# Output projection of an encoder layer: second norm scaled on ScalarE by halves, early weight operands spread evenly, an own bank for the mixed transposition's second half

## Chip, core and metric

The kernel runs on one core of a Trainium2 chip. The metric is the device time of one execution in microseconds, lower is better. Engines are named as in the profile: PE is TensorE's matrix multiplier and PEld its weight load, DVE is VectorE, ACT is ScalarE, POOL is GpSimd, SP is SyncE, which here issues nearly all loads (a q behind a name, as in SPq, means the engine's sequencer and its queue of DMA issues).

## The reference

One encoder layer over 1280 tokens (256 of a prompt, 1024 of a sample), width 1024, feed-forward width 2816, all in fp32:

```
proj = rmsnorm(x, attn_norm_g) @ w_in
a = mla_group(...)                 # latent attention, 8 heads, 512 columns
b = na_group(...)                  # neighbourhood attention, 8 heads, 512 columns
mix = concat(rmsnorm(a, mla_out_g), rmsnorm(b, na_out_g))
x = x + mix @ w_o                  # output projection
h2 = rmsnorm(x, ffn_norm_g)        # second norm
x = x + (silu(h2 @ w_gate) * (h2 @ w_up)) @ w_down
y = rmsnorm(x, final_norm_g)
```

## The kernel before

Every fp32 product is made of three matmuls on operands split into a high part (rounded to fp32r) and a low part (the rest): high x high, high x low, low x high. This is `mm3`, lines 111 to 113. The feed-forward products use a fast matrix multiplication scheme with 20 block products for each block of weights; their operands are sums and differences of 2 x 4 blocks of weights (W side) and of the activations (S and X tiles).

The change lies in the stage between attention and the feed-forward, and in the first block of feed-forward products. Tokens come in NT = 10 tiles of 128. The loop `for t in range(NT)` interleaves work of several tiles:

- `mix_in(t + 2)` loads a tile of attention results (`m`, from `a_d` and `b_d`) through SP, squares its two halves on ACT (L881, with the sums of squares), gets the reciprocal root `rm` on POOL (`rstd_of`, L90 and L92) and scales both halves on POOL (L886). `mixed[0]` is the last of these instructions.
- `mix_T(t + 1)` transposes the scaled tile on PE in two halves of four 128 x 128 blocks (L898) into the PSUM tile `trm`, of which there is one buffer. Each half is read by ACT for the high part (L900) and by DVE for the low part (L901) of `mT`.
- `out_proj(t)` does 16 groups of three matmuls (two halves of 512 columns, eight blocks of the inner dimension) into the PSUM tiles `po`; as each half ends, DVE adds the residual (L930, `added[0]`). Between its groups stand, by `between`, the transpositions of the next tile's `mT` (after groups 1 and 5) and those of the previous tile's second norm (after groups 10 and 13).
- `ffn_in(t)` squares the sum `x` on ACT (L941), stores `x` to `xm_d`, gets `rh` on POOL (`normed[0]`), and scales `x` into `h2` on DVE in one instruction of 1024 columns (L944, `scaled[0]`; `h2` has the tile name `m`). Its inner `half(q)`, called a tile later from `out_proj`, transposes four blocks each (L960): half 0 into `trh`, evicted by DVE (L964) with the gain, half 1 into a junk bank of the pool `pm0` ("M" in the profile, `junk[2]`) or for the last two tiles into `trm`, evicted by ACT (L970).
- `early_operands` is a generator that makes 18 weight operands of the first feed-forward block ahead of time on POOL: sums (L1067), the high part (L1072), the low part (L1074) into one of two buffers `wr`; SP stores each to `wop_d` (`load_r(*job)`, L77), at the start of the next iteration, or at once when three are pending. `next(early, None)` makes one. The raw weights (`wraw`) come in three parts in the first three iterations.
- `JOBS`, `FIRST` and `SECOND` are sums and splits of the S and X tiles on ACT and DVE (L985, L987, L995), placed behind named instructions.

Engine order: SP's queue and, from t = 1 to the end of the first feed-forward block, PE's order are the program's (`manual_schedule`). The other engines get their order from a planner that takes instructions by program order and its own estimate of when they are ready; `tc.issue_after(ins)` holds the instructions of a block behind `ins` on the same engine. Each engine executes its list in order.

After the loop, the first feed-forward block runs 20 steps (`SEQ0`), each with one product for G (gate) and one for U (up). At step `at` SP loads the operands for step `at + 3` into the ring `wr`; raw weights of the second block are loaded by `load_raw(1, ...)`. `xm_in(i)`, called within step 3, does the two halves of the last tile's transpositions; after the second it releases the pool `po` and opens `pm1`, from which the fifth step takes its banks. The pool `pm0` has four banks named M0, used as junk or transposition targets in the loop and by the products later.

Of the kernel before, what the change touches and what calls it, by code (L numbers as in the profile page):

```python
# [12 lines left out]
F32 = mybir.dt.float32  # L13
F32R = mybir.dt.float32r
AF = mybir.ActivationFunctionType
ALU = mybir.AluOpType
# [3 lines left out]
P = 128  # L20
# [20 lines left out]
def encoder_trunk(ctx: ExitStack, tc: tile.TileContext, x_tm, x_T, g_attn, w_c, w_v, w_qk,  # L41
# [3 lines left out]
    nc = tc.nc  # L45
# [10 lines left out]
    def pool(name, bufs=1, side=None, space=None):  # L56
        kw = {"reuse_waits": "tile"}
        if side:
            kw["side"] = side
        if space:  # L60
            kw["space"] = space
        return tc.alloc_tile_pool(name=name, bufs=bufs, **kw)

    def load(out, in_):
        nc.sync.dma_start(out=out, in_=in_)

    def store(out, in_):
        nc.scalar.dma_start(out=out, in_=in_)
# [7 lines left out]
    def load_r(out, in_):  # L76
        nc.sync.dma_start(out=out.bitcast(F32), in_=in_.bitcast(F32))  # L77
# [10 lines left out]
    def rstd_of(out, ss, n):  # L88
        w = out.shape[1]
        nc.gpsimd.tensor_scalar(out=out, in0=ss, scalar1=1.0 / n, scalar2=EPS,  # L90
                                op0=ALU.mult, op1=ALU.add)
        return nc.gpsimd.tensor_tensor(out=out, in0=out, in1=mhalf[:, 0:w], op=ALU.pow).ins  # L92
# [70 lines left out]
    def load_x(t):  # L163
        x = rx.tile([P, D], F32, name="x", bufs=2)
        load(x, x_tm[t * P:(t + 1) * P, :])
        return x
# [684 lines left out]
    po = pool("po", space=PSUM, side="right")  # L851
# [6 lines left out]
    def load_wo(n, pl, nm):  # L858
        raws = pl.tile([P, 2, D], F32, name=nm)
        for j in range(2):  # L860
            kc, raw = 2 * n + j, raws[:, j]
            load(raw, w_o[kc])
            nc.gpsimd.tensor_scalar(out=raw, in0=raw, scalar1=gm[:, kc:kc + 1], scalar2=1.0,
                                    op0=ALU.mult, op1=ALU.mult)
            wt = rw.tile([P, 2, D], F32R, name=f"wo{kc}")
            split_w(wt[:, 0], wt[:, 1], raw)
            wo.append(wt)
# [23 lines left out]
    def mix_T(t, mn):  # L891
        mT = (rt1 if t % 2 else rt0).tile([P, 2, KC, P], F32R, name=f"mT{t % 2}")

        def half(q):
            tr = po.tile([P, 4, P], F32, name="trm", bufs=1)
            for i in range(4):
                kc = 4 * q + i
                nc.tensor.transpose(tr[:, i], mn[:, kc * P:(kc + 1) * P], ident)  # L898
            hi, lo = mT[:, 0, 4 * q:4 * q + 4], mT[:, 1, 4 * q:4 * q + 4]
            last_split[0] = nc.scalar.copy(out=hi, in_=tr).ins  # L900
            last_low[0] = nc.vector.tensor_sub(out=lo, in0=tr, in1=hi).ins  # L901

        return mT, half
# [31 lines left out]
    normed, added = [None], [None]  # L935

    def ffn_in(t, x):
        h2 = rm.tile([P, D], F32, name="m", bufs=3)
        ss = rm.tile([P, 1], F32, name="ssh", bufs=2)
        r = rm.tile([P, 1], F32, name="rh", bufs=2)  # L940
        nc.scalar.activation(h2, x, AF.Square, accum_out=ss)  # L941
        store(xm_d[t], x)
        normed[0] = rstd_of(r, ss, D)
        scaled[0] = nc.vector.tensor_scalar(out=h2, in0=x, scalar1=r, scalar2=1.0, op0=ALU.mult,  # L944
                                            op1=ALU.mult).ins
        cuts, a = [], t * P
        while a < (t + 1) * P:
            j = a // XC
            e = min((j + 1) * XC, (t + 1) * P)
            cuts.append((j, slice(a - j * XC, e - j * XC), slice(a - t * P, e - t * P)))  # L950
            a = e

        def half(q):
            if q and t < NT - 2:
                tr = junk[2].rearrange("p (a b) -> p a b", a=4)
            else:
                tr = po.tile([P, 4, P], F32, name="trm" if q else "trh", bufs=1)
            for i in range(4):
                kc = 4 * q + i
                tp = nc.tensor.transpose(tr[:, i], h2[:, kc * P:(kc + 1) * P], ident)  # L960
            for j, to, of in cuts:
                if q == 0:
                    for k in range(2):
                        ev[0] = nc.vector.tensor_mul(  # L964
                            out=X[k, j][:, :, to], in0=tr[:, 2 * k:2 * k + 2, of],
                            in1=gf[:, 2 * k:2 * k + 2].unsqueeze(2).to_broadcast(
                                [P, 2, of.stop - of.start])).ins
                else:
                    for i in range(4):
                        nc.scalar.activation(X[2 + i // 2, j][:, i % 2, to], tr[:, i, of],  # L970
                                             AF.Copy, scale=gf[:, 4 + i:5 + i])
            return tp.ins

        return half

    ev, scaled = [None], [None]
# [56 lines left out]
    def load_raw(fp, i):  # L1033
        load(raw[:, i], src[i][fp])

    pm = [pool("pm0", space=PSUM)]
    for n, (pl, nm) in enumerate(((rw, "wo4"), (rw, "wo5"), (rw, "wo6"), (rt0, "mT0"))):
        load_wo(n, pl, nm)
    junk = [None] + [pm[0].tile([P, 512], F32, name="M0", bufs=4) for _ in range(2)]
    cur, half = mix_T(0, mix_in(0))  # L1040
    half(0)
    half(1)
# [36 lines left out]
    early = early_operands()  # L1079
# [3 lines left out]
    def behind_now(ins, job):  # L1083
        if job:
            with tc.issue_after(ins):
                job()
# [3 lines left out]
    for t in range(NT):  # L1090
        if t == 1:
            pe_order.enter_context(tc.manual_schedule(engines={mybir.EngineType.SP,
                                                               mybir.EngineType.PE}))
        if t + 2 < NT:
            with tc.issue_after(last_split[0]):
                coming = mix_in(t + 2)
        x = load_x(0) if t == 0 else x_next
        x_next = load_x(t + 1) if t + 1 < NT else None
        for job in kept:
            load_r(*job)  # L1100
        kept.clear()
        if t < 3:
            k = (slice(4, 6), slice(0, 4), slice(6, 8))[t]
            for i in range(2):
                load(raw[:, i, k], src[i][0][:, k])
        with tc.issue_after(mixed[0]):
            for _ in range(2 if 1 < t < 6 else 1):
                next(early, None)
        jobs = JOBS.get(t, (None,) * 3)
        halves_[0] = t < NT - 1  # L1110
        if t == NT - 1:
            with tc.issue_after(scaled[0]):
                for job in SECOND[4:5] + SECOND[6:]:
                    job()
        between = {}
        if t + 1 < NT:
            nxt, half_m = mix_T(t + 1, ahead)

            def second_m(half_m=half_m, jobs=jobs):
                half_m(1)  # L1120
                behind_now(last_low[0], jobs[0])

            between[1] = lambda: half_m(0)
            between[5] = second_m
        if t:
            def first_h(half=last_half, jobs=jobs):
                half(0)
                behind_now(ev[0], jobs[2])
                if t == 8:
                    behind_now(ev[0], jobs[3])  # L1130

            between[10 if t < 9 else 8] = first_h
            between[13 if t < 9 else 11] = lambda half=last_half: half(1)
        if t < NT - 1:
            between[7] = lambda jobs=jobs: behind_now(added[0], jobs[1])
        out_proj(t, cur, x, between)
        if t == NT - 1:
            break
        last_half = ffn_in(t, x)
        with tc.issue_after(normed[0]):  # L1140
            next(early, None)
            if t == 8:
                third_2(gps, slice(0, 168))
        cur, ahead = nxt, coming
# [14 lines left out]
    def xm_in(q):  # L1159
        last_half(q)  # L1160
        if q == 0:
            return
        for p_ in reversed(r3):
            p_.release()
        po.release()
        pm.append(pool("pm1", space=PSUM, side="right"))
        l4.append(pool("l4t"))
# [163 lines left out]
    for at in range(20):  # L1331
        if at and at + 3 < 20:
            load_r(ring[(at + 3) % 4], wop_d[SEQ0[at + 3][0]])
        if at in (5, 7):
            load_raw(1, at == 7)
        if at in BUILD:
            with tc.issue_after(evicted[0]):
                build_S(BUILD[at])
        w = ring[at % 4]
        for i, C in enumerate((G, U)):  # L1340
            product(C, chains[i], written[i], SEQ0, at, (w[:, 0, i], w[:, 1, i]), BANK.get(at))
            if at == 3:
                xm_in(i)
    pe_order.close()
    gate(G, 1)
# [438 lines left out]
```

## Time and profile before

| | us |
|---|---|
| three runs | 1592.95, 1595.09, 1591.53 (median 1592.95) |
| the profiled execution | 1593.86 |
| its span in the profile | 1591.8 |
| PE busy | 1559.4 (98% of the span) |
| DVE, ACT, POOL busy | 1016.4, 760.2, 766.4 |

The page gives one profiled execution. The times in its rows are counted from the start of the span. A row of the timeline gives start, length, engine, line, operation, tile written and tiles read, shape, number of instructions merged, and in brackets the idle time before it and what ended it. A row of the waits gives the waiting engine, tile and line, what it waited for, the total, how often, and the longest.

### The profile page before, as it was taken

To read this page: it belongs to the slowest core of one execution; us is meant where nothing else is said; L and a number is where in the kernel's file an instruction comes from. 1 tells how busy PE (TensorE), PEld (TensorE's weight loads), DVE (VectorE), ACT (ScalarE), POOL (GpSimd) and SP (SyncE) were. 2 spreads that over 40 slices of the span, in tenths; PEclk is the share of its full clock that TensorE was granted. 3 is DMA by queue.
4 is the path that set the end of the run, shared out by engine and by line. 5 is a ranking of instruction groups with operands and counts; after the bars stand their busy time and mean duration, and the time that the engine had idled before them with its cause. 6 is when DMAs were issued, how large, how long until landed. Compare 5 with 4: busy or idle time off the path is not lost.

```text
span 1591.8 us, 23991 instructions
## 1 busy us (share of the span) xinstructions
PE 1559.4 (98%) x8560; PEld 1394.9 (88%) x8560; DVE 1016.4 (64%) x1656; ACT 760.2 (48%) x1552; POOL 766.4 (48%) x961
## 2 busy tenths in 40 slices
PE   8999999999999999999999999999999999999998
PEld 8888789998888888877799999999999988888886
DVE  5754035556777777535698766566766666886676
ACT  6534144455777777633344344444334353443334
POOL 4632235544211119359626888788888871010002
PEclk9999999999999999999999999999999999999999
DMA  8626022243101021285573232223322237843434
GB/s 288 206 73 167 17 54 64 38 169 107 32 15 30 20 97 38 69 274 202 193 247 110 85 103 78 100 88 111 111 77 98 83 131 286 292 120 99 151 104 157
DMA packets 118022, 190.38 MB, mean 120 GB/s; under 512 B 34960, under 2 KB 65424, under 8 KB 115344
## 3 DMA queue, kind: packets, MB, share of 16 engines
q1 hardware_dynamic: 85216, 162.64, 31.4%
q10 hardware_dynamic: 31872, 23.14, 4.6%
q0 software_dynamic: 816, 3.08, 0.5%
q8 instruction: 67, 1.10, 0.3%
q14 instruction: 51, 0.42, 0.1%
HBM read 128.92 MB, written 59.90 MB: 119 GB/s over the span
## 4 chain that ended last, share of the span: by engine, by line
PE 83%; POOL 6%; DMA 3%; DVE 3%; ACT 3%; issue 2%; SPq 0%; POOLq 0%; ACTq 0%; DVEq 0%
PE M L113 10%; PE M L111 10%; PE M L112 10%; PE d L111 6%; PE d L113 6%; PE d L112 6%; PE o L789 4%; PE tp L779 3%; PE na_o L513 3%; PE pj L111 2%; PE pj L112 2%; PE pj L113 2%; PE S L111 2%; PE S L113 2%; PE S L112 2%
## 5 line engine op out<-in xcount | busy, mean ns | idle before, releaser
L1242 DVE TENSOR_TENSOR C<-M,C 128x428 f32<-128x428 f32 (+1 forms) x263 | 151.0, 594 | 144.0 <-issue 68.1
L1023 POOL TENSOR_TENSOR wr<-wt,wr 128x512 fp32r<-128x512 f32 (+1 forms) x106 | 148.9, 1405 | 67.4 <-ACT wr L1021 67.3
L1021 ACT CAST wr<-wt 128x512 fp32r<-128x512 f32 (+1 forms) x106 | 63.2, 599 | 134.2 <-PE M L112 123.7
L111 PE MATMUL M<-s,wr 128*128 128x428 f32 x352 | 125.9, 358 | 1.2 <-ACT x L970 1.2
L112 PE MATMUL M<-s,wr 128*128 128x428 f32 x352 | 125.4, 356 | 0.0
L113 PE MATMUL M<-s,wr 128*128 128x428 f32 x352 | 125.3, 357 | 0.0
L101 DVE TENSOR_TENSOR PT<-tp,PT 128x512 fp32r<-128x512 f32 (+1 forms) x144 | 93.4, 658 | 35.4 <-ACT PT L100 34.2
L1244 ACT COPY C<-M 128x428 f32<-128x428 f32 (+1 forms) x128 | 63.3, 514 | 84.6 <-PE M L113 84.6
L111 PE MATMUL M<-x,wr 128*128 128x428 f32 x264 | 94.2, 357 | 1.5 <-DVE C L1242 1.4
L100 ACT CAST PT<-tp 128x512 fp32r<-128x512 f32 (+1 forms) x144 | 79.4, 568 | 33.4 <-PE tp L779 30.2
L802 POOL TENSOR_TENSOR ob<-ob 128x128 f32<-128x128 f32 x40 | 18.4, 461 | 158.5 <-ACT ob L799 155.1
L771 DVE TENSOR_REDUCE mm<-S 128x1 f32<-128x1024 f32 (+1 forms) x80 | 85.0, 1062 | 13.8 <-PE S L113 12.3
L113 PE MATMUL M<-x,wr 128*128 128x428 f32 x264 | 91.5, 357 | 0.5 <-POOL wr L1023 0.3
L112 PE MATMUL d<-SE 128*128 128x512 f32 (+1 forms) x238 | 91.7, 387 | 0.0
L111 PE MATMUL d<-SE 128*128 128x512 f32 (+1 forms) x238 | 89.6, 388 | 0.0
L113 PE MATMUL d<-SE 128*128 128x512 f32 (+1 forms) x238 | 89.6, 387 | 0.0
L1284 ACT CAST SE<-as 128x640 fp32r<-128x640 f32 x58 | 42.2, 727 | 94.8 <-issue 57.2
L773 ACT ACTIVATE ex<-S,mm 128x1024 f32<-128x1024 f32 (+1 forms) x80 | 79.8, 998 | 14.9 <-DVE mm L771 13.6
L779 PE MATMUL tp<-ident,ex 128*128 128x128 f32 x544 | 79.2, 274 | 2.4 <-DVE PT L101 1.3
L789 PE MATMUL o<-PT,v 128*128 128x256 f32 x544 | 80.6, 287 | 0.8 <-ACT PT L100 0.8
L90 POOL TENSOR_SCALAR ry<-ssy 128x1 f32<-128x1 f32 x5 | 4.1, 820 | 157.6 <-ACT yo L1574 157.5
L111 PE MATMUL M<-SE,wr 128*128 128x428 f32 x220 | 78.6, 357 | 0.3 <-ACT C L1244 0.3
(466 smaller groups left out, 4909.1 us busy)
## 6 DMA issues: line engine op xcount, KB each, us to landing
as<-act_d SPq DMA_DIRECT2D x73, 320.0 KB
act_d<-C SPq DMA_DIRECT2D x70, 320.0 KB
w<-in_w_down_dram SPq DMA_DIRECT2D x44, 256.0 KB
x<-in_x_tm_dram SPq DMA_DIRECT2D x20, 512.0 KB
wr<-wop_d SPq DMA_DIRECT2D x20, 512.0 KB
wraw<-in_w_gate_dram SPq DMA_DIRECT2D x10, 1024.0 KB
wraw<-in_w_up_dram SPq DMA_DIRECT2D x10, 1024.0 KB
wop_d<-wr SPq DMA_DIRECT2D x18, 512.0 KB
```

Of the source, the lines that this page charges most:

```text
L100: i = nc.scalar.copy(out=hi, in_=ps)
L101: nc.vector.tensor_sub(out=lo, in0=ps, in1=hi)
L111: nc.tensor.matmul(out, lhsT=sh, rhs=mh, start=first, stop=False, **kw)
L112: nc.tensor.matmul(out, lhsT=sh, rhs=ml, start=False, stop=False, **kw)
L113: return nc.tensor.matmul(out, lhsT=sl, rhs=mh, start=False, stop=last, **kw).ins
L771: nc.vector.reduce_max(out=nm[:, u:u + 1], in_=S, axis=AX.X, negate=True)
L773: nc.scalar.activation(ex, S, AF.Exp, bias=nm[:, u:u + 1], scale=1.0, accum_out=l[:, u:u + 1])
L779: nc.tensor.transpose(tp[:, j], ex[:, kt * P:(kt + 1) * P], ident)
L789: nc.tensor.matmul(oT, lhsT=vv, rhs=pt[s][g][:, j], start=kt == 0 and s == 0, stop=kt == nkt - 1 and s == 1)
L1023: i1 = (eng or nc.gpsimd).tensor_tensor(out=lo, in0=raw_, in1=hi, op=SUB)
L1242: evicted[0] = nc.vector.tensor_add(out=o, in0=ps[:, 0:XN[j]], in1=o).ins
L1244: nc.scalar.copy(out=o, in_=ps[:, 0:XN[j]])
```

## The change

Six edits:

1. `ffn_in`: the scale of the second norm is two ACT instructions of 512 columns each instead of one DVE instruction of 1024.
2. `mix_T`: for tiles from 2 on, the second half is transposed into a third junk bank `junk[3]` (of the M0 banks of `pm0`) instead of the only buffer of `trm`.
3. The loop: one early operand behind `mixed[0]` in every iteration (before: two in iterations 2 to 5); behind `normed[0]` two in iterations 1 and 2, else one (before: one).
4. Iteration 9: the jobs `SECOND[4:5] + SECOND[6:]` stand behind `added[0]` instead of `scaled[0]`.
5. First feed-forward block: the raw weights of the second are loaded at steps 6 and 8 instead of 5 and 7.
6. `xm_in` is called within step 2 instead of 3.

```diff
 def mix_T(t, mn):
     ...
         def half(q):
-            tr = po.tile([P, 4, P], F32, name="trm", bufs=1)
+            if q and t > 1:
+                tr = junk[3].rearrange("p (a b) -> p a b", a=4)
+            else:
+                tr = po.tile([P, 4, P], F32, name="trm", bufs=1)
 ...
 def ffn_in(t, x):
     ...
         normed[0] = rstd_of(r, ss, D)
-        scaled[0] = nc.vector.tensor_scalar(out=h2, in0=x, scalar1=r, scalar2=1.0, op0=ALU.mult,
-                                            op1=ALU.mult).ins
+        for i in range(2):
+            hs = slice(i * 512, (i + 1) * 512)
+            scaled[0] = nc.scalar.activation(h2[:, hs], x[:, hs], AF.Copy, scale=r).ins
 ...
-    junk = [None] + [pm[0].tile([P, 512], F32, name="M0", bufs=4) for _ in range(2)]
+    junk = [None] + [pm[0].tile([P, 512], F32, name="M0", bufs=4) for _ in range(3)]
 ...
         with tc.issue_after(mixed[0]):
-            for _ in range(2 if 1 < t < 6 else 1):
-                next(early, None)
+            next(early, None)
 ...
         if t == NT - 1:
-            with tc.issue_after(scaled[0]):
+            with tc.issue_after(added[0]):
                 for job in SECOND[4:5] + SECOND[6:]:
                     job()
 ...
         last_half = ffn_in(t, x)
         with tc.issue_after(normed[0]):
-            next(early, None)
+            for _ in range(2 if t in (1, 2) else 1):
+                next(early, None)
 ...
     for at in range(20):
         if at and at + 3 < 20:
             load_r(ring[(at + 3) % 4], wop_d[SEQ0[at + 3][0]])
-        if at in (5, 7):
-            load_raw(1, at == 7)
+        if at in (6, 8):
+            load_raw(1, at == 8)
 ...
-            if at == 3:
+            if at == 2:
                 xm_in(i)
```

## Prediction

> **What bounds the kernel now.** I read the page first: busy shares, the granted clock, the chain that ended last.
>
> ```profile
> PE 1559.4 (98%) x8560; PEld 1394.9 (88%) x8560; DVE 1016.4 (64%) x1656; ACT 760.2 (48%) x1552; POOL 766.4 (48%) x961
> PEclk9999999999999999999999999999999999999999
> PE 83%; POOL 6%; DMA 3%; DVE 3%; ACT 3%; issue 2%; SPq 0%; POOLq 0%; ACTq 0%; DVEq 0%
> ```
>
> PE is busy 98% of the span at full clock, so an edit that leaves its matmuls alone can only win idle PE time. The change touches the output projection and the first feed-forward products, so I cut that stretch into windows, from one first transposition of the second norm (trh) to the next, then up to the first wait of the products. Columns: length, then PE, PEld, DVE, ACT, POOL busy with their counts, clock, DMA share, GB/s.
>
> ```profile
> 685.60:699.00 13.40, 12.97 (x65) 10.43 (x63) 3.67 (x7) 4.60 (x12) 5.86 (x9) 1.00 0.75 263
> 699.00:711.96 12.96, 12.96 (x65) 10.64 (x66) 3.94 (x7) 3.68 (x10) 9.52 (x13) 1.00 0.86 290
> 711.96:725.02 13.06, 12.97 (x65) 10.43 (x63) 5.16 (x8) 5.43 (x15) 11.67 (x15) 1.00 0.67 236
> 725.02:739.10 14.08, 13.12 (x64) 10.51 (x65) 6.17 (x12) 5.54 (x17) 13.46 (x16) 1.00 0.61 224
> 739.10:754.65 15.55, 13.45 (x65) 10.35 (x65) 9.41 (x14) 4.71 (x11) 14.77 (x16) 1.00 0.57 202
> 754.65:768.72 14.07, 13.38 (x65) 10.48 (x66) 10.28 (x15) 6.86 (x17) 13.29 (x14) 1.00 0.53 188
> 768.72:781.53 12.81, 12.81 (x65) 10.57 (x64) 8.05 (x15) 4.89 (x13) 5.80 (x9) 1.00 0.69 231
> 781.53:798.27 16.74, 16.65 (x81) 13.37 (x80) 10.28 (x16) 5.81 (x13) 10.11 (x15) 1.00 0.38 139
> ```
>
> Seven windows hold one token tile each, the same matmuls every time; I call the time in which PE works on out_proj for t tile t (699.00 lies in tile 2, 739.10 in tile 5), and trh there belongs to the norm of the tile before. The shortest, 12.81 us, has PE busy throughout: that is the floor. Together they take 95.93 us against 7 x 12.81 = 89.67, an excess of 6.26 us, and the worst three are those where POOL is busy 13.3 to 14.8 us. The last window loses nothing. The waits of PE from 675 to 900 us name the losers:
>
> ```profile
> PE trh L960 <- DVE m L944: 2.2, 3, 1.0
> PE M L111 <- ACT x L970: 1.2, 1, 1.2
> PE trm L898 <- DVE mT L901: 1.0, 2, 0.6
> PE M L111 <- DVE C L1242: 1.0, 1, 1.0
> PE trm L898 <- POOL m L886: 0.9, 1, 0.9
> ```
>
> Named idle time inside the seven tiles is 2.2 + 1.0 + 0.9 = 4.1 us of the 6.26; the rest is PE draining and refilling around each stall. I spread it in proportion (x1.52): late scale of the second norm 3.3, the mixed transposition's second half 1.6, its first half 1.4. The 1.2 us wait stands outside them, at the feed-forward products. What makes all three late is seen in the chain of waits (start, us, what) and the largest of SyncE's own waits from 670 to 800 us:
>
> ```profile
> 686.41 8.30 DMA wraw<-in_w_up_dram
> 694.88 0.63 POOL wr L1072
> 695.59 1.29 POOL wr L1074
> 697.25 0.57 POOL rh L92
> 707.32 3.66 DMA m<-a_d
> ```
> ```profile
> SPq L77 <- POOL wr L1074: 34.3, 12, 7.3
> ```
>
> So between about 686 and 764 us the chain that matters runs not over PE but over POOL, which makes early weight operands (L1067, L1072, L1074), to SyncE, which stores them in order, to the loads of the attention rows (m) queued behind those stores, to ACT's squares and back to POOL for the norm.
>
> **The change, part by part.**
>
> **1. Second norm's scale from DVE to ACT.** Now:
>
> ```profile
> L944 DVE TENSOR_SCALAR m<-x,rh x10: 735/1066/1770, 679.5 to 805.2; 128x1024 f32<-128x1024 f32 x10
> ```
> ```profile
> 736.69 0.56 POOL L92 TENSOR_TENSOR rh<-rh,mhalf 128x1 f32<-128x1 f32 x1
> ```
> ```profile
> 737.28 1.76 DVE L944 TENSOR_SCALAR m<-x,rh 128x1024 f32<-128x1024 f32 x1 [4.47 <-POOL rh L92]
> 738.97 0.68 DVE L901 TENSOR_TENSOR mT<-trm,mT 128x512 fp32r<-128x512 f32 x1
> ```
> ```profile
> 739.10 0.66 PE L960 MATMUL trh<-ident,m 128*128 128x128 f32 x4 [0.95 <-DVE m L944]
> ```
>
> DVE needs 0.74 us alone and up to 1.77 while POOL runs; the transpositions of the first half wait for all of it. [...] ACT's two halves are not in the trace; the nearest rows are its square of 128x512 and the square of 128x1024:
>
> ```profile
> 738.27 0.60 ACT L881 ACTIVATE M<-m 128x512 f32<-128x512 f32 x1 [2.99 <-DMA m<-a_d]
> 755.24 0.60 ACT L881 ACTIVATE M<-m 128x512 f32<-128x512 f32 x1 [4.21 <-DMA m<-a_d]
> 711.06 0.60 ACT L881 ACTIVATE M<-m 128x512 f32<-128x512 f32 x1 [5.03 <-DMA m<-a_d]
> ```
> ```profile
> L941 ACT ACTIVATE m<-x x10: 1058/1062/1108, 677.4 to 799.2; 128x1024 f32<-128x1024 f32 x10
> ```
>
> So 0.53 to 0.60 us a half; I take 0.60, the same shape. In the tile shown the first half would be ready at 737.28 + 0.60 = 737.9, before PE's 739.10 - 0.95 = 738.15: stall gone. [...] The norm of tile 1, transposed in tile 2's call, stays close: its r comes at 697.25 + 0.57 = 697.8, since L1072 there waited for a raw weight load, so 698.4 against PE ready at 699.00 - 0.43 = 698.57. Of 3.3 us I take 2.9 back. ACT gains 10 x 1.2 us of work; it is busy 4 to 7 us of each tile, so the work itself is hidden. What is not: ACT runs in order, and behind a scale waiting for POOL stand the high half of the mixed transposition (L900), the squares (L881) and the evictions L970. L900's low half (L901) already waits behind L944 on DVE today (738.97 above), and its product is used only in the next tile: nothing new there. If instead squares waiting for their load stand ahead of the scale, that is new: 0 at best, the slower rival below at worst. I take 0.6, near the floor, because with part 3 the loads come earlier.
>
> **2. Own bank for the second mixed transposition** (tiles 2 to 9).
>
> ```profile
> 749.77 0.63 PE L898 MATMUL trm<-ident,m 128*128 128x128 f32 x4 [0.41 <-DVE mT L901]
> 764.75 0.63 PE L898 MATMUL trm<-ident,m 128*128 128x128 f32 x4 [0.64 <-DVE mT L901]
> ```
>
> Both waits are for the first half's low part to be read out of the only bank. With the fourth M0 bank nothing is left to wait for: 1.6 us back. The feed-forward products take M0 banks only at 798 us, after the last use (about 779): cost nothing.
>
> **3. Early operands spread evenly.** 18 operands are made; now 2, 2, 3, 3, 3, 3, 2 per tile, then 2, 3, 3, and 2 in each of tiles 3 to 7. An operand is 0.63 + 1.29 us plus 1.3 per sum, so tiles 3 to 5 lose about 3.3 us of POOL each and fit 12.8. A further effect is in SyncE's order: the third operand of a tile forces a store out in mid-tile, ahead of the next m load; without it the m load is issued behind stores whose operands are long done, roughly half a tile sooner. First-half stalls (1.4 us) should go: I take 1.3. Tiles 6 and 7 now have POOL work, but the window 768.72 has 7 us free on it. The ring loads that follow on SyncE wait for the last two stores, some 8 us later than now but still ahead of 798: no cost.
>
> The price is at the front. Tile 1 now makes three operands; so the store of its first (done 695.59 + 1.29 = 696.9) moves ahead of the m load for tile 4:
>
> ```profile
> 701.25 1.37 POOL L886 TENSOR_SCALAR m<-m,rm 128x512 f32<-128x512 f32 x2
> ```
> ```profile
> 688.76 0.33 SPq L65 DMA_DIRECT2D m<-a_d  x1
> ```
>
> That load slips from 688.8 to about 697.2, lands 3.7 us later (row 707.32 above) at 700.9, two squares (1.4), r (1.0, as two steps of POOL) and half of L886's 1.37 follow, so the first half is normalized at about 704.1. PE transposes it now at
>
> ```profile
> 704.81 0.60 PE L898 MATMUL trm<-ident,m 128*128 128x128 f32 x4
> ```
>
> less the 0.6 gained before: 704.2. That just fits, but operand 8, whose buffer waits for that same store, can stand ahead of it on POOL: 0 to 2 us. The same can recur one tile on, with the last raw weights, 0 to 2.5. I take 1.2 of the possible 4.5: an exact fit leaves some spill, but both need the unlucky order.
>
> **4. Last tile's transpositions one step earlier.**
>
> ```profile
> 808.04 0.60 PE L960 MATMUL trm<-ident,m 128*128 128x128 f32 x4
> 809.88 0.46 PE L111 MATMUL M<-s,wr 128*128 128x428 f32 x1 [1.23 <-ACT x L970]
> ```
> ```profile
> 801.05 0.55 POOL L92 TENSOR_TENSOR rh<-rh,mhalf 128x1 f32<-128x1 f32 x1
> ```
>
> The fifth product needs a bank of the pool that is freed only when ACT has read these transpositions. One product pair (2.3 us of PE) put between covers the 1.23 plus 0.25 of refill. In turn the scale must be there by 804.1 instead of 806.4; r comes at 801.6 and ACT's two halves by 802.9, or later if evictions stand ahead of them. I take 1.4.
>
> **5. Nearly free.** The sums for the second block wait on the residual add instead of the scale: DVE starts them some 2 us sooner, in a window without loss. The next weights load one step (2.3 us) later:
>
> ```profile
> 841.07 1.29 POOL L1023 TENSOR_TENSOR wr<-wraw,wr 128x512 fp32r<-128x512 f32 x1 [16.41 <-ACT wr L1021]
> ```
>
> POOL idles 16.4 us between its first sums and the first split, so the cover is ample; without it each us late would show whole.
>
> Sum: 2.9 + 1.6 + 1.3 + 1.4 = 7.2 back, 0.6 + 1.2 = 1.8 given, net 5.4. The profiled execution took 1593.86 us (span 1591.8): 1588.5. The median of the three runs, 1592.95, is 0.9 lower, so I forecast 1587.6. Later PE time should shift along as it is, PE being the bound.
>
> **Rivals.** Changes within 0.2%, 3.2 us, are about what cannot be told from none.
>
> (a) New waits take what the old gave: the two front stalls at their full 4.5 us, and 0.6 on ACT. For it: in tile 1 POOL has to wait for the store of 696.9 before operand 8, with rm queued near. Against: only two of nine tiles. Gain 7.2 - 5.1 = 2.1, hence 1590.8. Chance 0.26.
>
> (b) Slower: ACT takes the squares ahead of the scale and they wait for loads that come no sooner. By the three ACT rows: in tile 5 squares end near 739.7, first half 740.3, against 738.15, a stall of 2.2; in tile 6, 755.24 + 1.5 + 0.6 = 757.3 against 753.8: 3.5; in tile 3 0.5; in tile 2, with the slipped load, 700.9 + 0.7 + 0.6 = 702.2 against 698.6: 3.6. That is 9.8 for today's 3.3, less 1.6 and 1.4 that still come back, first-half stalls unchanged: 3.5 slower, 1596.5. It takes all four tiles to cross the bound. Against it: a scale needs only r, which POOL has at 737.25, 2.5 us before the squares end in tile 5. Chance 0.12.
>
> (c) The forecast, gains of 3.3 to 7.7: chance 0.62. Its ceiling is the whole excess plus 1.5, and the 1.0 us wait on DVE's evictions in the feed-forward, if a lighter DVE clears it: 8.8.
>
> The range reaches from 1584.8 (gain 8.1) to 1593.0 (none), taking in (a) and leaving out (b) and some of the edge. Faster 0.62, same 0.26, slower 0.12.
>
> **What would show it.** Right: the tile windows after 725 us at 12.8 to 13.1; POOL near 11 us in each; no wait of trm on L901; no wait of M on L970; squares no longer waiting 3 us for m. Wrong: PE waiting on ACT's scale for more than 1 us in any tile, a new wait of trm on L886 near 704 or 717, POOL waiting for a store in tile 1, or the tiles clean and the gain lost after 812.

## Result and profile after

The changed kernel takes 1586.70 us (median of 6 runs, 1584.81 to 1587.47) beside 1594.03 of the kernel before (6 runs, 1591.53 to 1595.92): ratio 0.9953 with a 95% interval of 0.9940 to 0.9966, so 7.3 us less (5.4 to 9.6 by the interval). The forecast was 5.4 us less.

The profiled execution took 1584.81 us (span 1583.0), 8.8 under that of before in span. 1.1 of it is there already at the first trh, before any of the stalls (it stands at 684.48 instead of 685.60, and in the other kernels below at 684.7 to 687.9, so this is scatter). 6.06 lie in the seven tiles and 1.5 at the start of the feed-forward products: from the eighth trh to the same wait of M on DVE's eviction (867.70 before, 858.99 after) it is 86.17 against 84.64 us.

The busy shares on the page of after:

```profile
PE 1556.5 (98%) x8560; PEld 1394.9 (88%) x8560; DVE 1006.4 (64%) x1646; ACT 773.9 (49%) x1572; POOL 761.1 (48%) x961
```

The same windows as in the prediction, from one trh to the next, then to the products (length, then PE, PEld, DVE, ACT, POOL busy with counts, clock, DMA share, GB/s):

```profile
684.48:697.29 12.81, 12.81 (x65) 10.58 (x64) 2.13 (x4) 4.18 (x10) 5.82 (x9) 1.00 0.76 270
...
735.86:748.66 12.80, 12.80 (x65) 10.57 (x64) 7.31 (x12) 6.78 (x15) 12.01 (x14) 1.00 0.59 200
748.66:761.54 12.88, 12.88 (x65) 10.58 (x64) 6.91 (x11) 6.80 (x15) 11.77 (x15) 1.00 0.67 230
761.54:774.35 12.81, 12.81 (x65) 10.58 (x64) 7.39 (x11) 6.27 (x15) 9.04 (x10) 1.00 0.48 162
774.35:790.90 16.55, 16.46 (x80) 13.24 (x79) 9.17 (x17) 6.96 (x15) 9.98 (x18) 1.00 0.56 204
```

From 684.48 to 774.35 are 89.87 us, 0.20 over seven times 12.81, and PE is busy in all of it. No tile gives POOL more than 12.0 us, and the last of the seven has 9.0 us where it had 5.8. (Only tile 7 has new operands; by the counts that the prediction lists, tile 6 has two before and after.) The total is hardly smaller: the whole stretch in one window, before and after, has the same 86 POOL instructions.

```profile
685.60:781.53 95.93, 91.66 (x449) 73.42 (x448) 46.67 (x73) 35.71 (x92) 74.38 (x86) 1.00 0.66 232
```
```profile
684.48:774.35 89.87, 89.87 (x449) 74.05 (x448) 37.67 (x63) 45.45 (x106) 71.61 (x86) 1.00 0.69 235
```

Of the excess of 6.26 us before, 4.27 are idle time of PE (95.93 less 91.66) and 1.99 longer busy time (91.66 against 89.67): nearly all of what the prediction calls draining and refilling.

All waits of PE from 675 to 900 us that are left (two; the four rows on trh, trm and x are gone):

```profile
PE M L111 <- DVE C L1246: 1.0, 1, 1.0
PE M L111 <- ACT C L1248: 0.3, 1, 0.3
```

And ACT's waits for the attention rows from 675 to 800 us, first before, then after (total, times, longest): the loads are no longer late.

```profile
ACT M L881 <- DMA m<-a_d: 23.3, 6, 5.0
```
```profile
ACT M L881 <- DMA m<-a_d: 5.7, 4, 2.2
```

### The profile page after: what moved, and what is told of

Its sections match the earlier page's. It is cut to its first block, busy times and chain, and to the rows that moved or that the text cites. A ratio compares the mean times of both kernels' runs of the same rounds, so it can differ in the third digit from the quotient of the medians.

```text
span 1583.0 us, 23984 instructions
## 1 busy us (share of the span) xinstructions
PE 1556.5 (98%) x8560; PEld 1394.9 (88%) x8560; DVE 1006.4 (64%) x1646; ACT 773.9 (49%) x1572; POOL 761.1 (48%) x961
## 4 chain that ended last, share of the span: by engine, by line
PE 87%; DVE 3%; issue 3%; POOL 3%; ACT 2%; DMA 1%; SPq 0%; ACTq 0%; POOLq 0%; DVEq 0%
PE M L113 10%; PE M L112 10%; PE M L111 10%; PE d L111 6%; PE d L113 6%; PE d L112 6%; PE o L789 4%; PE tp L779 3%; PE na_o L513 3%; PE pj L111 2%; PE pj L112 2%; PE pj L113 2%; PE po L111 2%; PE po L113 2%; PE po L112 2%
## 5 line engine op out<-in xcount | busy, mean ns | idle before, releaser
L773 ACT ACTIVATE ex<-S,mm 128x1024 f32<-128x1024 f32 (+1 forms) x80 | 79.8, 998 | 14.9 <-DVE mm L771 13.6
```

Source lines behind the costliest of these rows:

```text
L773: nc.scalar.activation(ex, S, AF.Exp, bias=nm[:, u:u + 1], scale=1.0, accum_out=l[:, u:u + 1])
```

## Experiments

Two theories. A, the prediction's: each part brings its own booked gain. B: the tile stalls have one common cause, the early operands on POOL with the stores that SyncE puts between the loads, so that the spread alone removes them and the other parts find little left. The first eight kernels do one part alone, undo one, or leave two out (lean); the last four test how the spread works, and one wait that is left. "Seven tiles" is the time between the first and the eighth trh in the profile (no stall: 89.67); the last column is the median less that of the kernel before run beside it.

| kernel | seven tiles, us | ratio to before, 95% | us against before |
|---|---|---|---|
| before | 95.93 | | |
| changed | 89.87 | 0.9953 (0.9940 to 0.9966) | -7.3 |
| only_act | 98.44 | 1.0019 (1.0011 to 1.0028) | +3.1 |
| only_bank | 94.70 | 0.9997 (0.9988 to 1.0006) | -0.7 |
| only_spread | 89.87 | 0.9963 (0.9951 to 0.9976) | -5.7 |
| only_early | 96.94 | 1.0008 (0.9999 to 1.0017) | +1.4 |
| no_act | 89.86 | 0.9966 (0.9954 to 0.9979) | -5.4 |
| no_spread | 95.35 | 0.9990 (0.9981 to 0.9999) | -1.5 |
| no_early | 90.11 | 0.9954 (0.9942 to 0.9966) | -7.2 |
| lean | 89.88 | 0.9949 (0.9936 to 0.9963) | -7.6 |
| store_order | 101.56 | 1.0028 (1.0017 to 1.0040) | +5.4 |
| third_buffer | 97.42 | 1.0011 (1.0002 to 1.0020) | +2.4 |
| heavy | 90.52 | 0.9977 (0.9967 to 0.9987) | -3.9 |
| step13 | 89.88 | 0.9952 (0.9940 to 0.9965) | -7.5 |

**only_spread**: before, with edit 3 alone.

```diff
-            for _ in range(2 if 1 < t < 6 else 1):
-                next(early, None)
+            next(early, None)
...
-            next(early, None)
+            for _ in range(2 if t in (1, 2) else 1):
+                next(early, None)
```

> The kernel before with only the early operands spread evenly. Theory A (additive): 1.3 us faster, the waits on the second norm's scale (2.2 us idle) and on the single bank (1.0 us idle) stay. Theory B (common cause on POOL): most of the 6.26 us excess of the seven tile windows goes, 4 to 5.5 us faster, because r and the attention rows come in time and the low-part reading behind the DVE scale is no longer late.

The seven tiles take what they take in the changed kernel. Of the rows on trh, trm and x, one is left, and it lies outside the tiles:

```profile
PE M L111 <- ACT x L970: 1.2, 1, 1.2
```

DVE still scales in one instruction and trm has one buffer, and neither ever keeps PE waiting. This edit alone brings 5.7 us beside the 7.3 of the whole change, as B says (its range was 4 to 5.5).

**only_act**: before, with edits 1 and 4 (the sums of the last tile need something to stand behind).

```diff
-        scaled[0] = nc.vector.tensor_scalar(out=h2, in0=x, ...).ins
+        for i in range(2):
+            hs = slice(i * 512, (i + 1) * 512)
+            scaled[0] = nc.scalar.activation(h2[:, hs], x[:, hs], AF.Copy, scale=r).ins
```

> The kernel before with only the second norm's scale on ScalarE in two halves (and the sums of iteration 9 behind the residual add, which belongs to it). Theory A, the parts add up as the prediction booked them: the scale alone brings 2.9 us back, a time about 2.9 us below the kernel before. Theory B, one common cause, the backlog of early operands on POOL, which the other parts only avoid: r is still late and the attention loads are still late, so squares that wait for their load can stand ahead of the scale on ACT; the wait of the first second-norm transposition changes its name to ACT and the time is between 1 us faster and 3.5 us slower. The windows of tiles 5 and 6 (14.08 and 15.55 us before) tell: about 13 each by A, 14 or more by B.

Slower by 3.1 us. The waits of PE, and on its timeline the stalls of the scale and of the bank:

```profile
PE trm L898 <- DVE mT L901: 3.6, 1, 3.6
PE trh L961 <- ACT m L946: 1.8, 2, 1.1
```
```profile
712.18 0.60 ACT L881 ACTIVATE M<-m 128x512 f32<-128x512 f32 x1 [5.34 <-DMA m<-a_d]
712.81 1.32 ACT L946 ACTIVATE m<-x,rh 128x512 f32<-128x512 f32 x2
...
713.57 0.66 PE L961 MATMUL trh<-ident,m 128*128 128x128 f32 x4 [0.63 <-ACT m L946]
...
754.30 0.63 PE L898 MATMUL trm<-ident,m 128*128 128x128 f32 x4 [3.62 <-DVE mT L901]
```

The square that waits 5.34 us for its load ahead of the scale is rival (b)'s mechanism; it costs 1.8 us in two tiles, no more than DVE's lateness cost before (2.2). The loss is the other wait: the tile from 741.17 to 759.80 takes 18.63 us instead of 15.55, 3.1 more. What leads to it, on ACT and DVE:

```profile
739.97 1.34 ACT L946 ACTIVATE m<-x,rh 128x512 f32<-128x512 f32 x2 [3.63 <-POOL rh L92]
741.21 0.56 ACT L900 CAST mT<-trm 128x512 fp32r<-128x512 f32 x1
741.81 0.69 DVE L901 TENSOR_TENSOR mT<-trm,mT 128x512 fp32r<-128x512 f32 x1 [4.74 <-ACT mT L900]
...
747.30 2.63 DVE L996 TENSOR_TENSOR x<-x,x 128x428 f32<-128x428 f32 x2
749.97 0.91 ACT L986 CAST SE<-x 128x856 fp32r<-128x856 f32 x1 [6.81 <-DVE x L996]
```

The high half of the mixed transposition (L900) stands behind the scale on ACT, which waits for POOL's r; DVE waits 4.74 us for it, and its sums behind that (L988, L996) run late, the last in 2.63 us beside POOL's L1068 (747.84 to 749.47), where two of the same shape took 1.10 us at 745.61. ACT's next cast waits for those, and behind it stand the square and the next L900 (752.83), which must empty the only trm. One late r on POOL has gone through three queues before it reaches PE.

**only_bank**: before, with edit 2 alone.

```diff
-            tr = po.tile([P, 4, P], F32, name="trm", bufs=1)
+            if q and t > 1:
+                tr = junk[3].rearrange("p (a b) -> p a b", a=4)
```

> The kernel before with only the own bank for the second half of the mixed transposition (tiles 2 to 9). Theory A: the two bank waits go, 1.6 us faster. Theory B: PE comes that much earlier to the second norm's transpositions, whose operand is no earlier, and waits there instead: the bank waits go, the waits on the scale grow from 2.2 to about 3.2 us idle, and the time is within 0.6 us of the kernel before.

Not to be told from no change. The waits of PE show the bank's row gone and the scale's grown from 2.2, with a wait for a ring load that the kernel before does not have:

```profile
PE trh L963 <- DVE m L947: 2.7, 3, 1.5
PE M L111 <- DMA wr<-wop_d: 1.5, 1, 1.5
```

**only_early**: before, with edit 6 alone (`at == 3` to `at == 2`).

> The kernel before with only the last tile's transpositions one step earlier in the first feed-forward block. Both theories: the wait of 1.23 us on the eviction of the last transposition goes, 1.4 us faster, if the scale on DVE (before at 805.18 us, behind other work) comes 2.3 us earlier too. If it does not, PE waits for the scale at the third step instead: up to 1 us idle there, and at most 0.5 us faster.

At the interval's edge, no gain. The 1.23 us wait on L970 is gone, but the third step now waits for the scale itself, since DVE comes to it late behind the sums (L987) and the evictions (L1238, L1242):

```profile
807.99 0.74 DVE L944 TENSOR_SCALAR m<-x,rh 128x1024 f32<-128x1024 f32 x1
```
```profile
808.87 0.63 PE L960 MATMUL trh<-ident,m 128*128 128x128 f32 x4 [1.83 <-DVE m L944]
```

The seven tiles take 1.0 us more than before although this edit acts behind them, so where the loop stalls, one profiled execution can differ from another by about that much.

**no_spread, no_act, no_early**: the changed kernel with edit 3, the scale of edit 1, or edit 6 undone.

```diff
 no_spread
-            next(early, None)
+            for _ in range(2 if 1 < t < 6 else 1):
+                next(early, None)
...
-            for _ in range(2 if t in (1, 2) else 1):
-                next(early, None)
+            next(early, None)
 no_act
-        for i in range(2):
-            hs = slice(i * 512, (i + 1) * 512)
-            scaled[0] = nc.scalar.activation(h2[:, hs], x[:, hs], AF.Copy, scale=r).ins
+        scaled[0] = nc.vector.tensor_scalar(out=h2, in0=x, ...).ins
 no_early
-            if at == 2:
+            if at == 3:
```

> The changed kernel with the early operands back in their old places (two behind the mixture's norm in iterations 2 to 5). Theory A (the parts add up): it loses the 1.3 us booked for the spread, so about 1588 against 1586.7. Theory B (POOL's backlog is the cause, and the spread is what pays): attention loads come late again, so the squares stand in ACT's way; tile windows of 14 us or more come back, and the time lies between 1590 and 1597, with the single-bank wait of the scale-only kernel (3.6 us) gone or turned into a wait on ACT.

> The changed kernel with the second norm's scale back on DVE in one instruction. Theory A: the 2.9 us of late scales come back inside the tiles, about 1589.6. Theory B: all seven tile windows stay at 12.8 to 12.9 us, since r is no longer late; the only loss is at the third step of the first feed-forward block, where the transpositions now stand early and the scale comes late behind DVE's evictions: one wait of about 1.8 us, so 1588 to 1589.

> The changed kernel with the last tile's transpositions back in the fourth step. Both theories: the seven tile windows stay at 12.8 to 12.9 us and the one wait of 1.23 us on the eviction of the last transposition comes back: 1.4 to 1.5 us slower than the changed kernel, about 1588.1. If it is the same as the changed kernel, the wait was covered elsewhere.

Without the spread the tiles stall again, four times on ACT's scale, and all the other edits together bring only 1.5 us; first no_spread's row of the waits, then the one that no_act adds and the one that no_early adds to the two of the changed kernel:

```profile
PE trh L964 <- ACT m L949: 3.0, 4, 1.5
```
```profile
PE trh L963 <- DVE m L947: 1.6, 1, 1.6
```
```profile
PE M L111 <- ACT x L974: 1.2, 1, 1.2
```

With the spread and DVE's scale the loop is clean (89.86); the 1.6 us is the step that only_early showed, at 800.87. So what the ACT scale is good for here, by the trace, is that the early transpositions find their operand; the intervals of no_act and of the changed kernel overlap. For no_early the trace has the 1.2 us back, but the medians (-7.2 and -7.3) do not show it: a gain of this size is below what these runs resolve.

**lean**: before, with edits 1, 3, 4 and 6, without the bank and with the raw weights at their old steps.

> The kernel before with three of the edits alone: even spread, scale on ACT, last transpositions one step earlier; no own bank, next weights loaded where they were. Theory A: it loses the 1.6 us booked for the bank, about 1588.3. Theory B: as fast as the changed kernel, 1586.7 within 0.1%, and no wait of PE in the seven tiles, because with POOL in time the low part is read long before the second transposition.

No PE wait beyond the two of the changed kernel, the same tiles, the same time. The bank and the later raw weights bring nothing that shows beside the rest.

**store_order**: the changed kernel, with the spread, but each operand's store is forced as soon as the next operand is begun.

```diff
-            if len(kept) == 2:
+            if len(kept) == 1:
                 load_r(*kept.pop(0))
```

> The changed kernel, even spread kept, but each operand's store is forced out by the next operand, so that on SyncE the first operand of an iteration is stored ahead of the next load of attention rows, as the third operand did before. It separates the two things that the spread changes. If SyncE's order is what made the rows late: the loads of m slip again behind POOL's low parts, squares wait 3 us or more for them, waits of PE return in tiles 4 to 7, 1 to 4 us slower than the changed kernel. If the amount of POOL work per tile is what counts: the store is ready before the row's buffer is free, the windows stay at 12.8 to 12.9 us and the time at 1586.7 within 0.1%.

5.4 us slower than before, 12.7 slower than the changed kernel (at most 4 were expected), with POOL busy for only 66.5 us of the seven tiles. ACT's waits and PE's, then one round of the loop, on SyncE, ACT and POOL:

```profile
ACT M L881 <- DMA m<-a_d: 25.5, 7, 7.3
...
PE trm L901 <- POOL m L886: 8.8, 6, 2.5
```
```profile
713.70 0.38 SPq L65 DMA_DIRECT2D m<-a_d  x1
715.54 13.06 SPq L77 DMA_DIRECT2D wop_d<-wr  x2
717.37 0.60 ACT L881 ACTIVATE M<-m 128x512 f32<-128x512 f32 x1 [4.57 <-DMA m<-a_d]
720.52 0.19 POOL L90 TENSOR_SCALAR rm<-ssm 128x2 f32<-128x2 f32 x1 [5.31 <-ACT M L881]
721.60 1.37 POOL L886 TENSOR_SCALAR m<-m,rm 128x512 f32<-128x512 f32 x2
726.95 1.31 POOL L1078 TENSOR_TENSOR wr<-wt,wr 128x512 fp32r<-128x512 f32 x1
728.72 0.37 SPq L65 DMA_DIRECT2D m<-a_d  x1
```

Load, squares, norm, the operand behind the norm, its store, and only then the next load: 15.02 us in this round (13.6 to 15.0 in the others from 699 to 771 us), against 12.81 that PE needs for a tile. POOL stands idle 5.31 us in it, so this is the order of a queue and not an amount of work. The kernel before has the same loop in its three-operand tiles: a load at 734.94, the next at 750.35, 15.41 us, in a tile of 15.55. But store_order forces a store in every tile and the kernel before does not, so it shows that the loop by itself stalls PE, and not what the loop cost before.

**third_buffer**: before, with the old places, but a third operand buffer in free memory, so that a tile's third operand forces no store.

```diff
+    third = SE_t[:, 3424:4448].rearrange("p (a b c) -> p a b c", a=2, b=2)
-            if len(kept) == 2:
+            if len(kept) == 3:
-            w = ring[count[0] % 2]
+            w = (ring + [third])[count[0] % 3]
```

> The kernel before, with its three operands per iteration in 2 to 5, but a third buffer for them (in a part of the SE tile that is not yet in use), so that no store is forced out in mid-iteration: all three go out at the start of the next one, behind the loads of attention rows. Theory C (the loop through SyncE's order, load of m, squares, norm, first operand, its forced store, next load of m): the loop is cut, the waits of tiles 4 to 7 go although POOL has as much to do as before, 3.5 to 6 us faster than before. Theory D (too much POOL work per tile): POOL stays over 13 us in the tiles of 12.8 us, waits stay, 0 to 1.5 us faster.

The loop within a tile is cut: the wait for the loads halves, and no wait of PE on the norm (L886, here L887) is left. A load still stands behind the last store of the tile before: the one at 758.18 follows a store at 757.77, of an operand that POOL ends at 757.74. Yet the kernel is 2.4 us slower than before. ACT's row and PE's, then how the longest wait of PE comes about:

```profile
ACT M L882 <- DMA m<-a_d: 11.5, 5, 3.3
...
PE trm L899 <- DVE mT L902: 4.3, 2, 2.4
```
```profile
752.02 1.78 DVE L945 TENSOR_SCALAR m<-x,rh 128x1024 f32<-128x1024 f32 x1 [2.48 <-POOL rh L92]
...
764.06 0.57 ACT L901 CAST mT<-trm 128x512 fp32r<-128x512 f32 x1
764.65 0.69 DVE L902 TENSOR_TENSOR mT<-trm,mT 128x512 fp32r<-128x512 f32 x1 [1.74 <-ACT mT L901]
765.49 0.63 PE L899 MATMUL trm<-ident,m 128*128 128x128 f32 x4 [2.42 <-DVE mT L902]
```

In the two longest tiles (738.63 to 770.99) ACT waits for no load at all, but POOL is busy for 14.5 of 15.2 and 16.2 of 17.1 us, so r still comes late, DVE scales late and slowly (1.78 us at 752.02; the shortest scale of the kernel before took 0.735), and the lateness comes out at the bank. Freeing SyncE's order this far is not enough; the amount of POOL work per tile counts as well.

**heavy**: the changed kernel, with the low part of operands 9, 11, 13, 15 and 17 computed twice (the same result), 1.3 us of POOL more in each of five tiles.

```diff
+            if count[0] in (9, 11, 13, 15, 17):
+                nc.gpsimd.tensor_tensor(out=w[:, 1], in0=b[v], in1=w[:, 0], op=SUB)
```

> The changed kernel with the low part of the first operand of iterations 3 to 7 computed twice (1.3 us more POOL work in each of those tiles, the same result), which brings POOL from about 11.9 to 13.2 us a tile, what tiles 4 to 6 had before, with SyncE's order as changed. Theory C: no loop, POOL may run behind but the rows are loaded a tile ahead: within 1 us of the changed kernel's 1586.7. Theory D: the old waits return, 2 to 4 us slower.

3.4 us of the gain are lost, most of it in one wait of PE behind the seventh tile. ACT's waits for r, then the chain that ends in PE's wait:

```profile
ACT m L949 <- POOL rh L92: 22.7, 8, 4.6
```
```profile
774.63 1.34 ACT L949 ACTIVATE m<-x,rh 128x512 f32<-128x512 f32 x2 [4.52 <-POOL rh L92]
...
776.47 0.69 DVE L904 TENSOR_TENSOR mT<-M,mT 128x512 fp32r<-128x512 f32 x1 [5.63 <-ACT mT L903]
...
784.12 0.50 PE L111 MATMUL po<-wo,mT 128*128 128x512 f32 x1 [2.98 <-DVE x L933]
```

In the changed kernel ACT's waits for r sum to 12.7 us. It is the path of only_act again: a late r, the cast behind the scale on ACT, the low part and the sums on DVE, and at their end the residual add. POOL's busy time per tile reaches only 12.5 us, but it runs late: the scale starts 12.5 and 11.5 us after the first trh of the last two tiles (762.31, 774.63), in the changed kernel 7.5 and 7.4 (756.13, 768.93). So the even spread runs near POOL's limit: 12.0 us of 12.8 in its fullest tile hold, 1.3 more in each of five tiles do not.

**step13**: the changed kernel, with one eviction job of the first feed-forward steps moved (`11: (1,)` to `13: (1,)`), against the 1.0 us wait on DVE that is left.

> The changed kernel with one activation step of the first feed-forward output (step 1 of its seven) moved from the eleventh to the thirteenth product of the second block. It is meant for the one wait of PE left near there (1.0 us on DVE's eviction, at 859 us in the changed kernel's trace). If DVE's queue is late because of that step: the wait goes and 1.0 to 1.3 us are won, about 1585.5. If something else in DVE's queue is late: the wait stays or moves to the next product, no change.

Waits of 0.6 and 0.5 us on ACT and POOL take the place of the 1.0 and 0.3 us, so the second of the two expectations holds; the time is the changed kernel's within the interval. No kernel here is shown to beat the changed one; lean equals it with fewer edits.

## Why the prediction was right, and where its steps were not

The sum of the stalls was right. The gross gain of 7.2 us stands against 6.06 in the tiles and 1.5 at the products. PE was the bound, and its later work shifted along. The forecast fell 1.9 short, close to the 1.8 it gave away; the interval of the measured gain is too wide to make more of that. The booking by parts, theory A, was wrong nearly everywhere. That the total held all the same is in part luck: the 5.8 us booked to three parts (2.9, 1.6 and 1.3) came from one of them, which brings 5.7 alone, and all were made together. Of the scale or the bank alone, the same reasoning would have been wrong.

- **Spread: booked 1.3, brought 5.7.** The prediction named what makes all the stalls late (POOL, then SyncE's order, then the loads), and then gave this part only the first-half stalls. A late scale and a late bank are the same lateness one queue further on. Both of its effects, amount and order, count: even amounts with a forced store in each tile stall (store_order), and so do the old amounts with the order freed by a tile (third_buffer), or even ones with 1.3 us more (heavy). How much of the 5.7 each of the two brings stays open.
- **ACT scale: booked 2.9 less 0.6, alone 3.1 slower.** "Nothing new there" of L900 behind the scale is the step that failed: L901, and with it DVE's queue, waits for it. Rival (b) had the sign for this edit alone, by squares in front of the scale; its price of 9.8 in scale stalls was 1.8. A half took more than the 0.60 I chose from the squares' row:

```profile
L949 ACT ACTIVATE m<-x,rh x20: 705/712/729, 678.4 to 795.8; 128x512 f32<-128x512 f32 x20
```

  The median is 0.712 us. With the spread the ACT scale costs PE nothing in the tiles (busy for all of the 89.87 us), as r comes in time.
- **Bank: booked 1.6, nothing that shows on its own** (only_bank) and nothing beside the spread (lean).
- **Early transpositions: booked 1.4; 1.5 in the trace** (86.17 against 84.64 above), but only together with the ACT scale; the medians of the changed kernel and of no_early do not show it.
- **The front's price: booked 1.2, not paid.** POOL, SyncE and PE of the changed kernel:

```profile
693.69 1.29 POOL L1078 TENSOR_TENSOR wr<-wraw,wr 128x512 fp32r<-128x512 f32 x1
695.00 0.33 SPq L77 DMA_DIRECT2D wop_d<-wr  x1
695.43 0.38 SPq L65 DMA_DIRECT2D m<-a_d  x1
697.98 0.62 POOL L1076 TENSOR_SCALAR wr<-wraw 128x512 fp32r<-128x512 f32 x1
701.49 1.37 POOL L886 TENSOR_SCALAR m<-m,rm 128x512 f32<-128x512 f32 x2
703.01 0.60 PE L901 MATMUL trm<-ident,m 128*128 128x128 f32 x4
704.53 0.62 POOL L1076 TENSOR_SCALAR wr<-wraw 128x512 fp32r<-128x512 f32 x1 [1.68 <-DMA wop_d<-wr]
```

  The load does follow the forced store, at 695.43 where I took 697.2 (1.1 of that is the earlier start). The operand at 697.98 finds its buffer free; half of L886 is done at 702.2, and PE transposes at 703.01 without waiting. The wait for a store exists (1.68 us), but a tile later than the sign for being wrong had it, and behind the norm, where nobody is late for it.
- **The nearly free parts** cost nothing that can be seen.

Of the signs named ahead, those for right came: tiles at 12.80 to 12.88, POOL at 9.0 to 12.0 in those after 725 us (11 was named), no wait of trm on the low half or of M on the evictions of the last tile, squares waiting 2.2 us at most.

## What to carry to other kernels

When several engines wait in a chain of in-order queues, put down the stalls to the first queue of the chain, not one by one to the engines where they come out; test the edit there alone first (only_spread: 5.7 of the 7.3 us). Compare, per stage, the loop through an in-order DMA queue (load, work, forced store, next load) and the amount on the off-path engine with the bounding engine's time per tile; here PE stalled with a loop of 15.02 us against 12.81 (store_order) and with POOL busy for 16.2 of 17.1 us (third_buffer), and 12.0 of 12.8 us left no room for 1.3 more (heavy). Moving a late instruction to another engine moved the wait here to what was queued behind it there: in only_act DVE waited 4.74 us for the cast behind ACT's scale, and PE 3.62 us for the bank.

## What was not expected of the hardware

A stall cost nearly double here: one tile of third_buffer lost 4.33 us with a wait of 2.42. PE's clock, granted at 1.00 around it, falls to half after some gaps and not after others: one window of third_buffer behind its 2.42 us wait (0.50), and one of heavy behind its 2.98 us wait (1.00). The columns are those of the windows above, the clock third from the end.

```profile
767.00:769.00 2.00, 2.00 (x6) 1.56 (x5) 0.89 (x2) 0.36 (x2) 1.83 (x3) 0.50 0.56 86
```
```profile
784.10:786.00 1.90, 1.88 (x8) 1.56 (x9) 1.90 (x3) 1.15 (x2) 0.66 (x1) 1.00 0.90 198
```

In third_buffer that tile takes 17.14 us, 4.33 over the floor for a wait of 2.42: the rest, some 1.9, is mostly the half clock (PE is busy 14.72 us in that tile instead of 12.81, and its matmuls from 766.20 to 769.61 start 0.43 us apart instead of 0.23, 1.6 us more for the eight). The same belongs to only_act's tile (5.82 over, wait 3.62, clock 0.50 from 756 to 758) and to the longest of store_order (4.29 over, wait 2.52, clock 0.90 over the tile, matmuls 0.43 us apart from 708.14 to 709.85). The slow stretch stood behind gaps of 2.42, 2.52 and 3.62 us, while behind 2.98 us in heavy the clock stayed at 1.00 (to 790 us). The length of the gap alone does not sort these four, so what decides between them stays open here.
